# Rotary embedding at the eviction on VectorE, head norms with a scaled epsilon, and neighbourhood outputs folded out of PSUM

## The chip, the core and the metric

The kernel runs on one core of one Trainium2 chip. The time is the device time of one launch, in microseconds. Seven engines' records matter here: PE (TensorE matmul) and PEld (its weight loads), DVE (VectorE), ACT (ScalarE), POOL (GpSimd), SP (SyncE, which issues the DMAs), and the DMA queues themselves.

## What is computed

A trunk of two layers over 512 tokens (a grid of 8 rows by 64 columns) with 1024 channels in float32. Each layer adds three blocks to the residual stream, each behind an RMS norm: a mixer, a cross attention over 256 memory tokens, and a feed-forward block with a depthwise convolution. The change touches the mixer, which splits one input projection between eight heads of neighbourhood attention and grouped-query attention (eight query heads, two key heads, 64 channels each):

```python
proj = h @ w_in                                   # h = rms_norm(x)
na_q, na_k, na_v, g_q, g_k, g_v = split(proj)
na_out = neighbourhood_attention(na_q, na_k, na_v, rpb)
g_q = apply_axial_rope(rms_norm(g_q, q_norm), cos, sin)   # per head
g_k = apply_axial_rope(rms_norm(g_k, k_norm), cos, sin)
gqa_out = gqa_block_attention(g_q, g_k, g_v)
x = x + concatenate([na_out, gqa_out]) @ w_out

def rms_norm(x, g):
    return x * rsqrt(mean(x * x) + EPS) * g
def apply_axial_rope(x, cos, sin):                # halves x1, x2 of each axis
    return [x1 * cos - x2 * sin, x1 * sin + x2 * cos]
```

## The kernel before

Activations are held transposed: channels on the 128 partitions, the 512 tokens along the row. To keep float32 accuracy with TensorE's faster float32 replacement type, each operand is split in two parts, hi (a rounded copy, made on ACT) and lo (the rest, made on DVE or POOL), and a product is three matmuls: hi by hi, hi by lo, lo by hi. Every weight tile comes by DMA from SP's queue into a raw buffer, is cast to hi on ACT (line 265) and gets its lo on POOL or DVE (line 266), in two halves for most of the mixer's weights. There are four buffers of hi and lo, so a cast can wait for the matmuls that still read the weight four places before.

The RMS norm's factor of each token (`mix.rstd`, and `mix.rep`, the same spread over the partitions) is not put into the matmuls' operands; products are scaled by it as they leave PSUM.

*Order of the work.* PE, SP and a few other operations keep the order in which the program writes them. DVE, ACT and POOL are put in order by the tile scheduler, which has priorities and a simulated timeline; the order is fixed when the program is built, and each engine works through its own list in order. `behind(n)` shifts the priority of what it encloses.

*The mixer's loop.* Eight units of neighbourhood attention (four pairs of heads, two halves of the tokens each) are run by `weave`: in each round, transposes of the unit two rounds back, normalising of the one before, scores of the newest, and values of the unit two rounds back, with a piece of filler between. The filler is the rest of the input projection. For the grouped heads it is `gqa_project`, for k, q0, q1, v, q2, q3 in this order, each in two pieces of twelve matmuls; after that come the output projection and memory's keys and values. After the eight units, sixteen units of grouped attention follow in the same manner.

`Late` holds work to be done some pieces later: each piece is a tick, and `late(n, f)` runs f after n ticks.

*Values.* `na_values` multiplies with hi and lo of the probabilities side by side, and hi and lo of the values one below the other, so that a PSUM tile holds four parts to be added: two halves of the partitions, two along the row. Before, ACT copies the lower half (line 789), DVE adds it to the upper half for both parts (790), and a third addition in SBUF adds the two parts (791).

*Rotation.* `gqa_rope` takes the projected head pair out of PSUM (lines 840 to 842): ACT writes xs, the value by its gain, and its square, DVE writes cc, the value by gain and cosine. One piece later `swap` issues four DMAs that exchange the halves of xs into xr, sums the squares of each head by a matmul with `pairs`, and gets the variance on DVE (852, 855). Another piece later `rotate` has POOL take the power -1/2 (862), copy it into rows (863), multiply xr by the sine (864) and add cc (865). Two pieces later `norm` spreads the rows over the partitions by a matmul with the identity, and one piece later `split` multiplies xr by it (875) and makes the operands of the attention. The tables of cosine and sine are multiplied by `mix.rep` on POOL once in each layer (805), and the sums of squares by the square of `mix.rstd` (807).

Of the kernel before, what the change touches and what calls it, by code (L numbers as in the profile page):

```python
# [10 lines left out]
F32 = mybir.dt.float32  # L11
# [7 lines left out]
P = 128  # L19
# [154 lines left out]
def encoder_kernel(ctx: ExitStack, tc: tile.TileContext, t: dict, out: bass.AP):  # L174
# [203 lines left out]
    qkg = cpool.tile([P, DEPTH, 2], F32, name="qkg")  # L378
    gfin = cpool.tile([P, KC], F32, name="gfin")

    def load_parameters():
# [15 lines left out]
    def rsqrt(src, n, scale, factor=1.0):  # L397

        v = small(n)
        DVE.tensor_scalar(v, src, scale * factor, EPS * factor, op0=ALU.mult, op1=ALU.add)  # L400
        r = small(n)
        with behind(-40):
            POOL.tensor_tensor(r, v, mhalf[:, :n], op=ALU.pow)
        return r

# [10 lines left out]
    class Norm:  # L416
# [172 lines left out]
    for l in range(DEPTH):  # L589
# [185 lines left out]
        def na_values(u):  # L775
            p, bp = divmod(u, 2)
            pts = na.pop(u)
            if bp == 0:
                o32s[p] = tmp()
            th, tt = tmp((2, 2, P)), tmp((2, 2, P))  # L780
            for j in range(2):
                po = ps_mm().rearrange("p (i n q) -> p i n q", i=2, n=2)
                for i in range(2):
                    b = 2 * bp + i
                    for c in range(2):
                        PE.matmul(po[:, i], vblk[p // 2][WIN[b] + P * c][:, 2 * (p % 2) + j, :],
                                  pts[j][:, :, (2 * i + c) * P : (2 * i + c + 1) * P], start=c == 0, stop=c == 1)
                r = slice(64 * j, 64 * j + 64)
                ACT.copy(th[r], po[64:128])
                DVE.tensor_add(tt[r], po[0:64], th[r])  # L790
            DVE.tensor_add(o32s[p][:, 256 * bp : 256 * bp + 256].rearrange("p (i q) -> p i q", i=2), tt[:, :, 0], tt[:, :, 1])
            if bp == 1:
# [7 lines left out]

        gq, gk, gvt, gtab, r2 = [None] * 4, [], [], [], []

        def gqa_tables():
            for i in range(2):
                POOL.tensor_mul(gtab[0][:, i], gtab[0][:, i], mix.rep)
            r2.append(small(NB))
            POOL.tensor_mul(r2[0], mix.rstd, mix.rstd)

# [26 lines left out]
        def gqa_rope(g, pm):  # L835

            gain = qkg[:, l, 0:1] if g != "k" else qkg[:, l, 1:2]
            xs, sq, cc = tmp(), tmp(), tmp()
            with behind(-20):
                ACT.activation(xs, pm, AF.Copy, scale=gain)  # L840
                ACT.activation(sq, pm, AF.Square)
                DVE.scalar_tensor_tensor(cc, pm, gain, gtab[0][:, 0], op0=ALU.mult, op1=ALU.mult)  # L842

            def swap():
                xr = tmp()
                for i in range(4):
                    SP.dma_start(xr[32 * i : 32 * i + 32], xs[32 * (i ^ 1) : 32 * (i ^ 1) + 32])
                pv = ps_t()
                for b in range(NB):
                    PE.matmul(pv[:, 2 * b : 2 * b + 2], sq[:, b * P : (b + 1) * P], pairs, start=True, stop=True)  # L850
                v = small(2 * NB)
                DVE.tensor_tensor(v.rearrange("p (b j) -> p b j", j=2), pv[:, 0 : 2 * NB].rearrange("p (b j) -> p b j", j=2),
                                  r2[0].unsqueeze(2).to_broadcast([P, NB, 2]), op=ALU.mult)

                DVE.tensor_scalar(v, v, *((1.0 / HD, EPS) if g == "k" else (1.0, EPS * HD)), op0=ALU.mult, op1=ALU.add)
                late(1, lambda: rotate(xr, v))

            def rotate(xr, v):
                r = small(2 * NB)
                rows = tmp()  # L860
                with behind(-40):
                    POOL.tensor_tensor(r, v, mhalf[:, : 2 * NB], op=ALU.pow)
                    POOL.tensor_copy(rows.rearrange("p (b d) -> p b d", d=HD), r.unsqueeze(2).to_broadcast([P, 2 * NB, HD]))
                POOL.tensor_mul(xr, xr, gtab[0][:, 1])
                POOL.tensor_add(xr, cc, xr)
# [165 lines left out]
        def na_quanta(s):  # L1031
            if s == 3:
                gtab.append(rtile((2, S), F32))
                SP.dma_start(gtab[0], t["rope"])
                gqa_tables()
            return [NA_FILL] * 3
# [267 lines left out]
def _rope_tables():  # L1304

    tok = np.arange(S)
    col, row = tok // ROWS, tok % ROWS
# [69 lines left out]
```

## Time and profile before

| | |
|---|---|
| median of 3 runs | 1388.41 us (1386.73 to 1388.48) |
| the profiled execution | 1388.67 us |
| its span, first to last instruction | 1386.4 us |
| granted TensorE clock, mean | 0.992 of full speed |
| PE busy | 1355.3 us (98% of the span) |
| DVE, ACT, POOL busy | 838.3, 703.8, 719.7 us |

In the rows of the profile, `mm<-xg,hi` says which tiles an instruction writes and reads (mm, sc and tr are PSUM tiles; xg, r, t, s, hi, lo, raw are SBUF tiles), and L77 is a line of the kernel, which can be that of a helper. In a row of the timeline the first number is the start in us from the span's start, the second the duration; the bracket at its end is the idle time of the engine just before, and what ended it. In a row of groups the number behind x is how often it ran; then come the busy time in us, the mean of one in ns, and the idle time before them with what ended it. A float32 matmul with a plain float32 operand is recorded as two passes, so that four matmuls appear as eight. The clock (PEclk) is that granted to TensorE, as a share of full speed.

### The profile page before, as it was taken

Reading aid. Unit: us, or ns where it says so; the run is one execution under the profiler, and the core shown is the slowest. Engines: PE = TensorE matmul, PEld = TensorE weight load, DVE = VectorE, ACT = ScalarE, POOL = GpSimd, SP = SyncE. Lnnn points to the kernel's source line nnn. Section 1 sums busy time; section 2 is a strip of 40 time slices with the busy share of each in tenths; the row PEclk is TensorE's granted clock in tenths of the full one; section 3 lists DMA queues with packets and bytes.
Section 4 is the critical chain, followed back from the end, with each engine's and each line's share of the span. In section 5 each row is a group of like instructions: output and inputs, shape, how many; then the busy total and the mean of one; then the engine's idle time right before and its main releaser. Section 6 shows DMA issues by size and latency. Waiting matters only on the chain.

```text
span 1386.4 us, 19225 instructions
## 1 busy us (share of the span) xinstructions
PE 1355.3 (98%) x7072; PEld 1157.1 (83%) x7072; DVE 838.3 (60%) x1462; ACT 703.8 (51%) x1305; POOL 719.7 (52%) x537
## 2 busy tenths in 40 slices
PE   8999999999999999999999989999999999999997
PEld 7898789787888888888888978898788888888897
DVE  6666666363787187358446557754638833861874
ACT  6766577655443144234557657766654422432441
POOL 2458876635444444444645678756264444444441
PEclk9999999999999999999999999999999999999998
DMA  7753312322333333333356523223133333333331
GB/s 213 202 145 86 86 57 78 92 62 61 106 97 102 91 94 95 101 100 89 109 147 166 139 74 99 62 75 109 54 90 100 91 104 94 90 93 107 95 89 61
DMA packets 218205, 138.83 MB, mean 100 GB/s; under 512 B 6016, under 2 KB 211072, under 8 KB 218112
## 3 DMA queue, kind: packets, MB, share of 16 engines
q1 hardware_dynamic: 217968, 137.60, 34.9%
q8 instruction: 56, 0.92, 0.3%
q14 instruction: 37, 0.30, 0.1%
q10 hardware_dynamic: 144, 0.00, 0.0%
HBM read 125.00 MB, written 2.10 MB: 92 GB/s over the span
## 4 chain that ended last, share of the span: by engine, by line
PE 88%; ACT 4%; DVE 3%; POOL 2%; DMA 2%; issue 1%; SPq 0%; DVEq 0%; ACTq 0%; POOLq 0%
PE mm L77 79%; PE sc L77 5%; PE tr L64 3%; PE tr L77 1%; ACT hi L265 1%; DMA raw<-in_w_in 1%; POOL lo L266 1%; DMA raw<-in_w_down 1%; DVE s L900 1%; POOL r L266 0%; DMA xT<-in_xT 0%; ACT t L902 0%; DVE t L455 0%; DVE xg L473 0%; ACT t L745 0%
## 5 line engine op out<-in xcount | busy, mean ns | idle before, releaser
L266 POOL TENSOR_TENSOR lo<-raw,hi 128x1024 fp32r<-128x1024 f32 (+2 forms) x268 | 499.7, 1876 | 496.0 <-ACT hi L265 476.0
L77 PE MATMUL mm<-xg,hi 128*128 128x512 f32 x1920 | 595.5, 391 | 1.4 <-DVE t L842 1.4
L77 PEld LDWEIGHTS mm<-xg,hi 128*128 128x128 f32 x1920 | 357.4, 188 | 73.3 <-DVE t L842 1.6
L265 ACT CAST hi<-raw 128x512 fp32r<-128x512 f32 (+2 forms) x276 | 224.5, 837 | 349.0 <-PE mm L77 277.5
L77 PE MATMUL mm<-xg,lo 128*128 128x512 f32 x960 | 374.3, 390 | 0.0
L77 PE MATMUL mm<-r,hi 128*128 128x512 f32 (+1 forms) x1144 | 333.9, 376 | 4.4 <-ACT t L444 2.2
L77 PEld LDWEIGHTS mm<-r,hi 128*128 128x128 f32 x1144 | 209.2, 190 | 42.7 <-ACT t L444 3.1
L1202 DVE SCALAR_TENSOR_TENSOR t<-t,par,t 128x7 f32<-128x7 f32 (+1 forms) x352 | 201.9, 641 | 34.0 <-ACT t L1195 34.0
L77 PE MATMUL mm<-r,lo 128*128 128x512 f32 (+1 forms) x572 | 214.3, 375 | 0.0
L77 PEld LDWEIGHTS mm<-xg,lo 128*128 128x128 f32 x960 | 180.7, 188 | 38.1
L77 PEld LDWEIGHTS mm<-r,lo 128*128 128x128 f32 x572 | 108.5, 190 | 19.1
L1187 DVE TENSOR_TENSOR t<-mm,rep 128x512 f32<-128x512 f32 x88 | 60.1, 687 | 78.2 <-PE mm L77 62.3
L479 POOL TENSOR_SCALAR t<-t,s 128x512 f32<-128x512 f32 (+1 forms) x112 | 66.1, 607 | 75.1 <-DVE s L908 37.2
L1204 ACT ACTIVATE t<-t 128x512 f32<-128x512 f32 x44 | 27.9, 633 | 134.5 <-DVE t L1202 134.5
L1208 DVE TENSOR_TENSOR r<-t,r 128x512 fp32r<-128x512 f32 x44 | 90.5, 2056 | 7.3 <-ACT r L1207 4.1
L1231 DVE TENSOR_TENSOR xT<-xT,mm 128x512 f32<-128x512 f32 x32 | 21.9, 685 | 106.8 <-PE mm L77 106.8
L77 PE MATMUL sc<-r,r 128*128 128x256 f32 (+1 forms) x352 | 71.3, 334 | 0.4 <-ACT t L902 0.3
L64 PE MATMUL tr<-ident,t 128*128 128x128 f32 x456 | 63.3, 275 | 8.5 <-DVE r L473 2.8
L1195 ACT ACTIVATE t<-t,par 128x512 f32<-128x512 f32 x88 | 66.8, 806 | 3.2 <-DVE t L1187 3.2
L64 PEld LDWEIGHTS tr<-ident,t 128*128 128x128 f32 x456 | 52.0, 141 | 18.7 <-issue 6.9
L77 PE MATMUL mm<-r,r 128*128 128x256 f32 (+1 forms) x428 | 62.1, 297 | 0.1
L77 PEld LDWEIGHTS mm<-r,r 128*128 128x128 f32 x428 | 56.1, 191 | 2.7 <-POOL r L266 0.3
(155 smaller groups left out, 1598.8 us busy)
## 6 DMA issues: line engine op xcount, KB each, us to landing
raw<-in_w_up SPq DMA_DIRECT2D x88, 512.0 KB, 3.9
raw<-in_w_in SPq DMA_DIRECT2D x33, 512.0 KB, 4.5
raw<-in_w_down SPq DMA_DIRECT2D x32, 448.0 KB, 3.8
raw<-in_w_mem_kv SPq DMA_DIRECT2D x16, 512.0 KB, 3.9
raw<-in_w_down SPq DMA_DIRECT2D x16, 512.0 KB, 4.2
r<-in_bias SPq DMA_DIRECT2D x16, 384.0 KB, 6.2
r<-r SPq DMA_DIRECT2D x22, 256.0 KB, 5.3
raw<-in_w_out SPq DMA_DIRECT2D x8, 512.0 KB, 3.6
```

What stands on the lines that cost most here:

```text
L64: return lambda *a, **k: self.tc.keep_in_program_order(op(*a, **k))
L77: return self.tc.keep_in_program_order(self.engine.matmul(out, lhsT, rhs, **k))
L265: act.copy(hi[:, k], raw[:, k])
L266: (POOL if eng[0] == "P" else DVE).tensor_sub(lo[:, k], raw[:, k], f(hi)[:, k])
L479: eng.tensor_scalar(e, e, sums[:, col : col + 1], 1.0, op0=ALU.mult, op1=ALU.mult)
L900: DVE.tensor_reduce(nmx[:, c], sc[j], axis=AX.X, op=ALU.max, negate=True)
L1187: DVE.tensor_mul(u, us[side], ffn.rep)
L1195: ACT.activation(cc, u, AF.Identity, bias=par[:, l, CB + ch : CB + ch + 1], scale=w[1])
L1202: DVE.scalar_tensor_tensor(cc[:, dst], u[:, src], wi, cc[:, dst], op0=ALU.mult, op1=ALU.add)
L1204: ACT.activation(cs[0], cs[0], AF.Silu)
L1208: DVE.tensor_sub(acts[j][1], cs[0], f(acts[j][0]))
L1231: DVE.tensor_add(xT[m], xT[m], pm)
```

## The change

The signs of the sine table are exchanged between the halves, so that the sine is multiplied in before the halves change places. DVE now writes both xs (value by gain and sine) and cc from PSUM, and ACT only the square. `swap` issues the DMAs alone; the sums of the squares and the variance move into `rotate`, one piece later. The tables are no longer multiplied by the token's norm: since the head norm divides by the head's own size, the token's factor cancels but for the epsilon, which is multiplied by the token's variance instead (`geps`, made once in each layer by two operations on DVE). The variance then takes one operation on DVE instead of two. POOL keeps the power, the copy into rows and one addition for each group.

In `na_values` ACT copies only one of the two parts of the lower half, DVE adds the upper half's other part to it, and then the upper half's first part; both read PSUM, one after the other. As the diff has it, the copied part is the first of the lower half, the two parts of the upper half are added, and the lower half's second part, which multiplies lo by lo, is left out.

```diff
+    geps = cpool.tile([P, 2, NB], F32, name="geps")
...
         with behind(-40):
             POOL.tensor_tensor(r, v, mhalf[:, :n], op=ALU.pow)
-        return r
+        return r, v
...
-            self.rstd = rsqrt(pv[:, 0:nb], nb, 1.0 / D, factor)
+            self.rstd, self.var = rsqrt(pv[:, 0:nb], nb, 1.0 / D, factor)
...
-            th, tt = tmp((2, 2, P)), tmp((2, 2, P))
+            th = tmp((2, 2, P))
+            o32 = o32s[p][:, 256 * bp : 256 * bp + 256].rearrange("p (i q) -> p i q", i=2)
...
-                ACT.copy(th[r], po[64:128])
-                DVE.tensor_add(tt[r], po[0:64], th[r])
-            DVE.tensor_add(o32s[p][:, 256 * bp : 256 * bp + 256].rearrange("p (i q) -> p i q", i=2), tt[:, :, 0], tt[:, :, 1])
+                ACT.copy(th[r, :, 0], po[64:128, :, 0])
+                DVE.tensor_add(th[r, :, 1], po[0:64, :, 1], th[r, :, 0])
+                DVE.tensor_add(o32[r], po[0:64, :, 0], th[r, :, 1])
...
-        def gqa_tables():
-            for i in range(2):
-                POOL.tensor_mul(gtab[0][:, i], gtab[0][:, i], mix.rep)
-            r2.append(small(NB))
-            POOL.tensor_mul(r2[0], mix.rstd, mix.rstd)
+        def gqa_eps():
+            for i, e in enumerate((EPS, EPS * HD)):
+                DVE.tensor_scalar(geps[:, i], mix.var, e, None, op0=ALU.mult)
...
             with behind(-20):
-                ACT.activation(xs, pm, AF.Copy, scale=gain)
+                DVE.scalar_tensor_tensor(xs, pm, gain, gtab[0][:, 1], op0=ALU.mult, op1=ALU.mult)
+                DVE.scalar_tensor_tensor(cc, pm, gain, gtab[0][:, 0], op0=ALU.mult, op1=ALU.mult)
                 ACT.activation(sq, pm, AF.Square)
-                DVE.scalar_tensor_tensor(cc, pm, gain, gtab[0][:, 0], op0=ALU.mult, op1=ALU.mult)
             def swap():
                 xr = tmp()
                 for i in range(4):
                     SP.dma_start(xr[32 * i : 32 * i + 32], xs[32 * (i ^ 1) : 32 * (i ^ 1) + 32])
+                late(1, lambda: rotate(xr))
+
+            def rotate(xr):
                 pv = ps_t()
                 for b in range(NB):
                     PE.matmul(pv[:, 2 * b : 2 * b + 2], sq[:, b * P : (b + 1) * P], pairs, start=True, stop=True)
-                v = small(2 * NB)
-                DVE.tensor_tensor(v..., pv..., r2[0].unsqueeze(2).to_broadcast([P, NB, 2]), op=ALU.mult)
-                DVE.tensor_scalar(v, v, *((1.0 / HD, EPS) if g == "k" else (1.0, EPS * HD)), op0=ALU.mult, op1=ALU.add)
-                late(1, lambda: rotate(xr, v))
-
-            def rotate(xr, v):
-                r = small(2 * NB)
+                v, r = small(2 * NB), small(2 * NB)
+                DVE.scalar_tensor_tensor(v..., pv..., 1.0 / HD if g == "k" else 1.0,
+                    geps[:, int(g != "k")].unsqueeze(2).to_broadcast([P, NB, 2]), op0=ALU.mult, op1=ALU.add)
                 rows = tmp()
                 with behind(-40):
                     POOL.tensor_tensor(r, v, mhalf[:, : 2 * NB], op=ALU.pow)
                     POOL.tensor_copy(rows..., r.unsqueeze(2).to_broadcast([P, 2 * NB, HD]))
-                POOL.tensor_mul(xr, xr, gtab[0][:, 1])
                 POOL.tensor_add(xr, cc, xr)
                 late(2, lambda: norm(xr, rows))
...
-    tab = np.stack([np.concatenate([c, c, c, c]), np.concatenate([-s, s, -s, s])], axis=1)
+    tab = np.stack([np.concatenate([c, c, c, c]), np.concatenate([s, -s, s, -s])], axis=1)
```

More of the change, by code (lines that the diff above doesn't have):

```diff
@@ L797, in na_values @@
                     vblk[p // 2] = None
-        gq, gk, gvt, gtab, r2 = [None] * 4, [], [], [], []
-        def gqa_tables():
-            for i in range(2):
-                POOL.tensor_mul(gtab[0][:, i], gtab[0][:, i], mix.rep)
-            r2.append(small(NB))
-            POOL.tensor_mul(r2[0], mix.rstd, mix.rstd)
+        gq, gk, gvt, gtab = [None] * 4, [], [], []
+        def gqa_eps():
+            for i, e in enumerate((EPS, EPS * HD)):
+                DVE.tensor_scalar(geps[:, i], mix.var, e, None, op0=ALU.mult)
         def gqa_project(g):
@@ L850, in swap @@
                     PE.matmul(pv[:, 2 * b : 2 * b + 2], sq[:, b * P : (b + 1) * P], pairs, start=True, stop=True)
-                v = small(2 * NB)
-                DVE.tensor_tensor(v.rearrange("p (b j) -> p b j", j=2), pv[:, 0 : 2 * NB].rearrange("p (b j) -> p b j", j=2),
-                                  r2[0].unsqueeze(2).to_broadcast([P, NB, 2]), op=ALU.mult)
-                DVE.tensor_scalar(v, v, *((1.0 / HD, EPS) if g == "k" else (1.0, EPS * HD)), op0=ALU.mult, op1=ALU.add)
-                late(1, lambda: rotate(xr, v))
-            def rotate(xr, v):
-                r = small(2 * NB)
+                v, r = small(2 * NB), small(2 * NB)
+                DVE.scalar_tensor_tensor(
+                    v.rearrange("p (b j) -> p b j", j=2), pv[:, 0 : 2 * NB].rearrange("p (b j) -> p b j", j=2),
+                    1.0 / HD if g == "k" else 1.0, geps[:, int(g != "k")].unsqueeze(2).to_broadcast([P, NB, 2]),
+                    op0=ALU.mult, op1=ALU.add)
                 rows = tmp()
@@ L1034, in na_quanta @@
                 SP.dma_start(gtab[0], t["rope"])
-                gqa_tables()
+                gqa_eps()
             return [NA_FILL] * 3
```

## The prediction

> **What bounds the kernel now.** I read the page's busy shares and its chain first, then the chain in order of time, then windows of the two stretches where it leaves the matmuls, and there the timelines of PE and POOL.
>
> ```profile
> PE 1355.3 (98%) x7072; PEld 1157.1 (83%) x7072; DVE 838.3 (60%) x1462; ACT 703.8 (51%) x1305; POOL 719.7 (52%) x537
> PE 88%; ACT 4%; DVE 3%; POOL 2%; DMA 2%; issue 1%; SPq 0%; DVEq 0%; ACTq 0%; POOLq 0%
> 350.56 342.76 PE mm L77 x1512
> 835.30 0.92 PE sc L77 x4
> ```
>
> TensorE is the bound: a long stretch without a break does 1512 matmuls in 342.76 us, 0.227 us each, so a piece of twelve costs 2.72 us. The change adds and removes no matmul. It can only move time where PE waits, or where its clock is low after waiting. Those places are near the rotation:
>
> ```profile
> core 0: us, PE busy (x) PEld busy (x) DVE busy (x) ACT busy (x) POOL busy (x), PEclk, DMA share, GB/s
> 120.00:150.00 30.00, 26.64 (x149) 22.86 (x149) 18.88 (x34) 18.15 (x37) 23.59 (x22) 0.93 0.38 99
> 810.00:840.00 30.00, 26.76 (x145) 22.53 (x144) 17.90 (x31) 15.21 (x31) 23.13 (x22) 0.94 0.41 113
> ```
>
> POOL is busy 23 of 30 us there, and the clock falls to 0.93 and 0.94. PE's waits in layer 0 (times below 200) and layer 1, in brackets who ended them:
>
> ```profile
> 101.45 0.63 PE L64 MATMUL tr<-ident,t 128*128 128x128 f32 x4 [0.24 <-DVE s L852]
> 134.14 0.66 PE L64 MATMUL tr<-ident,t 128*128 128x128 f32 x4 [0.87 <-DVE r L473]
> 143.44 1.05 PE L77 MATMUL tr<-pairs,t 128*128 128x2 f32 x8 [1.26 <-ACT t L841]
> 146.75 2.08 PE L77 MATMUL mm<-ident,t 128*128 128x128 f32 x8 [1.24 <-POOL t L863]
> 148.48 1.20 PE L77 MATMUL mm<-r,hi 128*128 128x512 f32 x2
> 153.12 1.05 PE L77 MATMUL mm<-ident,t 128*128 128x128 f32 x8
> ...
> 801.46 0.73 PE L77 MATMUL mm<-xg,hi 128*128 128x512 f32 x2 [1.43 <-DVE t L842]
> 820.06 0.63 PE L64 MATMUL tr<-ident,t 128*128 128x128 f32 x4 [1.91 <-DVE r L473]
> 821.23 0.94 PE L77 MATMUL mm<-xg,hi 128*128 128x512 f32 x2
> 824.87 0.95 PE L77 MATMUL tr<-pairs,t 128*128 128x2 f32 x8
> 831.86 1.05 PE L77 MATMUL tr<-pairs,t 128*128 128x2 f32 x8 [1.33 <-ACT t L841]
> 838.78 1.15 PE L77 MATMUL mm<-ident,t 128*128 128x128 f32 x8
> ```
>
> The waits add up to 3.61 us and 4.67 us. From 821.23 to 824.87 the nine matmuls left of a piece take 3.64 us where 2.04 is usual: 1.6 us lost to a half-rate clock behind the 1.91 us wait. The spread in layer 0 costs 1.0 us (2.08 against 1.05) and more behind it.
>
> **The change, part by part.** The rows of the operations that it touches, and of their nearest kin:
>
> ```profile
> L842 DVE SCALAR_TENSOR_TENSOR t<-mm,qkg,r 128x512 f32<-128x512 f32 x10 | 7.5, 751 | 16.7 <-ACT t L841 14.6 <-POOL t L479 2.0
> L840 ACT ACTIVATE t<-mm,qkg 128x512 f32<-128x512 f32 x10 | 6.9, 695 | 0.1
> L841 ACT ACTIVATE t<-mm 128x512 f32<-128x512 f32 x10 | 6.0, 598 | 0.0
> L855 DVE TENSOR_SCALAR s<-s 128x8 f32<-128x8 f32 x10 | 4.6, 464 | 0.3
> L790 DVE TENSOR_TENSOR t<-mm,t 64x512 f32<-64x512 f32 x32 | 21.8, 683 | 10.7 <-ACT t L789 8.1 <-POOL t L479 1.5 <-POOL t L865 0.5
> L791 DVE TENSOR_TENSOR t<-t 128x256 f32<-128x256 f32 x16 | 9.7, 604 | 0.3
> L789 ACT COPY t<-mm 64x512 f32<-64x512 f32 x32 | 18.6, 583 | 6.1 <-PE mm L77 5.4
> L488 DVE TENSOR_TENSOR t<-mm,t 64x256 f32<-64x256 f32 x32 | 13.4, 418 | 11.2 <-ACT t L486 9.6 <-PE mm L77 0.7 <-PE tr L64 0.7
> L486 ACT COPY t<-mm 64x256 f32<-64x256 f32 x32 | 11.8, 369 | 4.3 <-PE mm L77 3.8
> L864 POOL TENSOR_TENSOR t<-t,r 128x512 f32<-128x512 f32 x10 | 12.9, 1295 | 3.4 <-DVE r L473 2.7 <-DMA t<-t 0.8
> L805 POOL TENSOR_TENSOR r<-r,rep 128x512 f32<-128x512 f32 x4 | 5.1, 1300 | 0.1
> ```
>
> *Engine totals.* POOL loses ten sine products (12.9 us), four table products (5.1) and two tiny squares. ACT loses ten evictions (6.9) and 32 x 0.21 us on smaller copies (583 against 369 ns for half the columns). DVE gains ten evictions of 0.75 us and four tiny products for the scaled epsilon, loses L855 (4.6), and per unit of neighbourhood values does 4 x 0.42 = 1.67 us where it did 2 x 0.68 + 0.60 = 1.97. None of these engines is the bound, so the totals are worth nothing by themselves. The epsilon products stand on DVE between the variance and the first scaling, which waits for the replicated norm anyway: nothing. If that cover were gone, two tiny operations a layer at L855's mean come to 4 x 0.46 = 1.9 us at most.
>
> *The values.* The chain that frees a product's PSUM tile was 0.58 + 0.68 = 1.27 us and is 0.37 + 2 x 0.42 = 1.20: nothing.
>
> *Eviction order.* The projection's PSUM tile is read by one engine after the other: before ACT, ACT, DVE (L842 waited 14.6 us for L841), now DVE, DVE, ACT. DVE no longer stands behind ACT, which begins with the weight cast at that moment. Three waits hang on that. 101.45: the sums' tile is read a piece later, and the transposes do not stand behind it: -0.24. 134.14 and 820.06: transposes wait for the split at L473, which stood behind L842 and so behind ACT's cast (1.14), 0.69 and 0.50. Now it stands behind two evictions, 1.5 us after the projection, and ACT's own half (cast, then a 0.6 us copy: 1.75). The split ends 2.4 us after the projection. In layer 0 PE gets there after some 2.8 us (turn, identity, values, four transposes): the 0.87 goes. In layer 1 there are no values between, PE gets there after 1.8: 0.7 of the 1.91 stays, -1.2, and with a wait no longer than layer 0's 0.87 I take the half rate behind it as gone: -1.6. Bounds of this pair: 0 to -3.5. 801.46: the tile is free after the square instead of after L842; ACT has the cast, a normalising copy of 0.4 and then the square, 2.8 us after the projection, where PE (two small groups and the values) is ready at 2.5: 0.3 stays, -1.1, bounds 0 and -1.4. The swap's four DMAs a group are issued in the same place of SP's queue, and what they read is ready earlier.
>
> *Sums a piece later.* The matmul over the squares, DVE's variance, POOL's power and the copy into rows now run two pieces ahead of the identity matmul that needs the rows, where there were three. For k and the first two q groups I find some 0.6 to 3 us to spare on POOL. The third q group is different: its sums come after the last projection piece, and on POOL, in the built program's order, its power now stands behind the pair of weight splits that this piece's end releases. Before, it had long run (first row below):
>
> ```profile
> 139.55 1.65 POOL L862 TENSOR_TENSOR s<-s,mhalf 128x8 f32<-128x8 f32 x1 [5.97 <-DVE s L855]
> 142.40 2.51 POOL L266 TENSOR_TENSOR lo<-raw,hi 128x512 fp32r<-128x512 f32 x2
> 150.76 1.36 POOL L479 TENSOR_SCALAR t<-t,s 128x512 f32<-128x512 f32 x2
> 829.65 1.29 POOL L500 TENSOR_TENSOR r<-t,r 128x512 fp32r<-128x512 f32 x1 [1.69 <-PE mm L77]
> 830.89 2.50 POOL L266 TENSOR_TENSOR lo<-raw,hi 128x512 fp32r<-128x512 f32 x2
> 833.33 0.62 POOL L863 COPY t<-s 128x512 f32<-128x512 f32 x1
> ...
> 141.05 1.14 ACT L265 CAST hi<-raw 128x512 fp32r<-128x512 f32 x2 [4.50 <-PE mm L77]
> 829.47 1.14 ACT L265 CAST hi<-raw 128x512 fp32r<-128x512 f32 x2
> ```
>
> The cast marks the end of the last piece, T: 141.05 and 829.47. Layer 0: half a cast 0.6, two splits 2.5, power 1.65, copy 0.62: rows at T + 5.4. PE has the sums, values and scores (0.8 + 0.9 + 0.92): it waits 2.7 us for the identity matmul. It waited 2.5 in two parts. The next identity matmul (fourth q group) hangs on POOL too: normalising 1.36, split 1.29, add 1.29, power, copy and some 0.4 of waiting for the normaliser's sums, at T + 12.0; or on PE at a low clock, T + 12.4. Before, it began at T + 12.07. One sum of 0.8 us has moved from before T to after it, so that compares with T + 12.87: -0.5, bounds -0.9 and +1. The low clock there I keep as it is.
>
> Layer 1: the split of the last neighbourhood output comes first, 1.25, then 2.5, 1.65, 0.62: rows at T + 6.0. PE has 0.8 + 0.92 + six matmuls 1.36 = 3.1: a new wait of 2.9 us in place of 1.33. The fourth group's rows follow after 1.38, 1.29, 1.65, 0.9 (two of memory's products now stand ahead) and 0.62: T + 11.85. Before, 838.78 - 829.47 = 9.31, and with the moved 0.8, 10.1: +1.75, bounds +0.5 and +2.5.
>
> *The clock behind that wait.* 1.91 us at 820.06 was followed by half rate at 1.6 us; 1.33 at 831.86 by none. 2.9 is nearer the first, but the second's surroundings (scores, output matmuls) are the ones that it has: 0 to 1.6, I take 0.8. [...]
>
> *Sum.* -0.24 - 0.87 - 0.5 - 1.1 - 1.2 - 1.6 + 1.75 + 0.8 = -3.0 us. The profiled execution took 1388.67 us (span 1386.4, 2.3 us around it), the median of the runs is 1388.41, 0.26 less. 1388.67 - 3.0 = 1385.7 against the profile, **1385.4** against the median.
>
> **Rivals.** *The clock holds behind the new waits.* Layer 1 loses no 0.8, and layer 0's half rate (2.08 for 1.05, then matmuls at 148.48 of 1.20 for 0.63, some 2.8 us in all) goes in part; for it speaks that 1.33 us cost no clock. POOL's chain to the fourth rows then is the bound, so only some of it counts: 1383 to 1384.6. [...]
>
> *Nothing changes.* The waits are only handed on: what is gained upstream is waited for at the third group's rows, since POOL's order there is fixed by the weight splits, or later, by the mixed stage of memory and grouped heads. For it: the sum is of eight terms of both signs. Against: the splits are released by PE and come earlier with it. 1388.4, within 1.5.
>
> *Slower: the rows come late for the second q group as well.* I have 0.6 us to spare there in both layers. If POOL is one split pair (2.5 us) behind, PE waits 1.9 us more in each, and with half rate behind them (1.6 each) that is +7.0: 1392.4. It decides against the change from some 1.5 us of lag in both layers. For it: POOL was at 23.6 of 30 us; against: 1.3 us a group leave that queue.
>
> **How the numbers follow.** 0.2% is 2.8 us, about what a measurement of this kernel can tell from none. The sum as taken 0.40: its own range is 1383.5 to 1387.5, a little over half beyond 0.2% (0.24) and the rest within (0.16). Clock holds 0.18, faster. Nothing changes 0.14. Slower 0.28, more than its margin says, because a tightened chain on a loaded in-order queue has more ways to be late than the one that I priced. Faster 0.42, same 0.30, slower 0.28. The range 1381.8 to 1392.0 reaches to the loss of both layers' low clock (-6.6) and most of the late second group.
>
> **What would show it.** PE's waits at L473, L842 and L841 of the list gone or under 0.8 us; the clock of layer 1's window at 818 to 825 full; a wait of 2.5 to 3 us at the identity matmul after the last projection in both layers, ended by POOL's copy; DVE's evictions ahead of ACT's square by 1.5 us. Wrong would be: identity waits also earlier, a clock under 0.9 in either window, or waits at the values.

## The result, and the profile after

The changed kernel took 1382.52 us (median of five runs, 1381.12 to 1384.26), the kernel before 1388.41 (1386.73 to 1388.80). By the medians that is 5.9 us less. The ratio, estimated from all the runs, is 0.9965, with a 95% interval of 0.9954 to 0.9976: 3.3 to 6.4 us faster. A second comparison, beside the experiments (e8 below), gave 0.9978, from 0.9967 to 0.9990. The forecast was 1385.4 us, faster, with a range of 1381.8 to 1392.0.

The profiled execution of the changed kernel took 1381.12 us, with a span of 1379.3. First its engine totals, from the page:

```profile
PE 1348.9 (98%) x7072; PEld 1153.1 (84%) x7072; DVE 836.7 (61%) x1482; ACT 691.4 (50%) x1295; POOL 701.4 (51%) x521
```

TensorE does the same 7072 matmuls in 1348.9 us where it took 1355.3. That is the first surprise of the page: its idle time (span less busy) has hardly moved, 1379.3 - 1348.9 = 30.4 us against 1386.4 - 1355.3 = 31.1. The matmuls themselves took 6.4 us less. Most of that is the clock: the profiled run has three stretches of 3.4 us at half clock fewer (the table below counts them), and at half clock such a stretch loses 1.7 us of matmul time, 5.1 us in all (worked out from one of before: from 251.33 to 254.74 us, 3.41 us, its granted clock was 0.50). The clock does not explain the other 1.3 us. The same two stretches as in the prediction, in the view of engine use by stretch (columns: stretch, length, busy time of each engine with its instructions, granted clock, DMA share, GB/s):

```profile
120.00:150.00 30.00, 25.77 (x157) 22.26 (x157) 18.61 (x35) 15.10 (x30) 22.95 (x22) 1.00 0.40 116
810.00:840.00 30.00, 25.11 (x139) 21.06 (x139) 19.24 (x34) 16.62 (x36) 22.35 (x27) 0.94 0.29 88
```

Layer 0's clock went from 0.93 to 1.00; layer 1's stayed at 0.94. Now PE's timeline, the rows of the rotation that begin with a wait (in brackets: idle time and who ended it):

```profile
143.01 1.16 PE L77 MATMUL mm<-ident,t 128*128 128x128 f32 x8 [2.59 <-POOL t L865]
149.44 1.16 PE L77 MATMUL mm<-ident,t 128*128 128x128 f32 x8 [1.64 <-POOL t L865]
...
813.23 0.66 PE L64 MATMUL tr<-ident,t 128*128 128x128 f32 x4 [0.57 <-DVE r L474]
826.24 1.16 PE L77 MATMUL mm<-ident,t 128*128 128x128 f32 x8 [2.66 <-POOL t L865]
```

Seven waits have become four: 8.28 us in the rotation of both layers before (3.61 + 4.67), 7.46 now (4.23 + 3.23). The waits for the projection's eviction and for ACT's square are gone. In their place PE waits for the third group's rows in both layers. POOL's timeline shows why, first layer 0, then layer 1:

```profile
138.14 2.54 POOL L266 TENSOR_TENSOR lo<-raw,hi 128x512 fp32r<-128x512 f32 x2 [2.92 <-ACT hi L265]
140.63 1.66 POOL L864 TENSOR_TENSOR s<-s,mhalf 128x8 f32<-128x8 f32 x1
142.35 0.61 POOL L865 COPY t<-s 128x512 f32<-128x512 f32 x1
...
820.13 1.28 POOL L501 TENSOR_TENSOR r<-t,r 128x512 fp32r<-128x512 f32 x1 [3.09 <-ACT r L500]
821.36 2.55 POOL L266 TENSOR_TENSOR lo<-raw,hi 128x512 fp32r<-128x512 f32 x2
823.87 1.65 POOL L864 TENSOR_TENSOR s<-s,mhalf 128x8 f32<-128x8 f32 x1
825.58 0.61 POOL L865 COPY t<-s 128x512 f32<-128x512 f32 x1
```

The power (L864) and the copy into rows (L865) stand behind the pair of weight splits (L266), after POOL had been idle for 2.92 us in layer 0 and 3.09 us in layer 1: the engine had time for them, but its inputs came too late.

### The profile page after: what moved, and what is told of

The parts are those of the page before. It is cut to its first block, busy times and chain, and to the rows that moved or that the text cites. A ratio compares the mean times of both kernels' runs of the same rounds, so it can differ in the third digit from the quotient of the medians.

```text
span 1379.3 us, 19221 instructions
## 1 busy us (share of the span) xinstructions
PE 1348.9 (98%) x7072; PEld 1153.1 (84%) x7072; DVE 836.7 (61%) x1482; ACT 691.4 (50%) x1295; POOL 701.4 (51%) x521
## 4 chain that ended last, share of the span: by engine, by line
PE 85%; DVE 2%; ACT 2%; POOL 1%; issue 0%; DVEq 0%; ACTq 0%; POOLq 0%
PE mm L77 77%; PE sc L77 4%; PE tr L64 3%; PE tr L77 1%; DVE xg L474 0%; DVE s L901 0%; ACT hi L265 0%; ACT xg L439 0%; DVE t L542 0%; POOL lo L266 0%; ACT t L903 0%; ACT t L1083 0%; ACT xg L473 0%; DVE r L1252 0%; POOL s L864 0%
## 5 line engine op out<-in xcount | busy, mean ns | idle before, releaser
L266 POOL TENSOR_TENSOR lo<-raw,hi 128x1024 fp32r<-128x1024 f32 (+2 forms) x268 | 498.9, 1874 | 513.3 <-ACT hi L265 507.5
```

The lines of the kernel that those rows point to most:

```text
L266: (POOL if eng[0] == "P" else DVE).tensor_sub(lo[:, k], raw[:, k], f(hi)[:, k])
```

## The experiments

The theory that the prediction left: the gain comes from the order of eviction (DVE first, no longer behind ACT's weight cast); the later sums lose some of it at the third group's rows; the fold and the epsilon are worth nothing. Rivals: the later sums carry the gain, or the fold does, or POOL's shorter work. Twelve runs were made, of ten new kernels, the changed kernel once more (e8) and e4 once more (e12), in groups of four (e1 to e4, e5 to e8, e9 to e12), each beside its own runs of the kernel before. That kernel took 1386.4 to 1387.0 us beside them, 1.4 to 2.0 us less than beside the changed kernel at first, so a forecast in us is better compared by its ratio to 1388.4. This is the key to all of them. "Waits" is the sum of PE's waits of 0.15 us and over in the profiled run, from the first group's sums to the fourth group's identity matmul, both layers together; "half rate" is the number of stretches of 3.4 us at half clock in it, ahead of the last 20 us.

| run | what it is | ratio to before (95%) | waits, us | half rate | profiled run, us |
|---|---|---|---|---|---|
| before | | 1 | 8.28 | 4 | 1388.67 |
| after | all parts | 0.9965 (0.9954 to 0.9976) | 7.46 | 1 | 1381.12 |
| e8 | all parts, again | 0.9978 (0.9967 to 0.9990) | 5.80 | 3 | 1382.21 |
| e1 | before + fold | 1.0017 (1.0008 to 1.0026) | 9.63 | 3 | 1387.62 |
| e2 | before + sine at eviction | 0.9962 (0.9949 to 0.9974) | 6.40 | 2 | 1382.07 |
| e3 | before + sums later | 1.0051 (1.0037 to 1.0064) | 10.44 | 4 | 1391.25 |
| e9 | before + fold + sine | 0.9968 (0.9955 to 0.9980) | 5.02 | 2 | 1380.39 |
| e10 | before + fold + sums later | 1.0078 (1.0066 to 1.0091) | 13.38 | 7 | 1397.84 |
| e5 | after without the fold | 1.0003 (0.9993 to 1.0013) | 8.75 | 6 | 1389.82 |
| e7 | after, ACT's square first | 1.0023 (1.0015 to 1.0032) | 11.19 | 2 | 1387.99 |
| e4 | after, all sums early | 0.9947 (0.9935 to 0.9960) | 4.34 | 1 | 1376.36 |
| e12 | e4 again | 0.9945 (0.9932 to 0.9957) | 6.01 | 1 | 1378.47 |
| e6 | after, third group's rows early | 0.9970 (0.9959 to 0.9981) | 6.45 | 4 | 1383.34 |
| e11 | after, only the fourth's sums late | 0.9972 (0.9962 to 0.9983) | 6.69 | 2 | 1384.38 |

Take the waits and 1.7 us a stretch off the profiled times, and 1370.1 to 1374.3 us are left in all fourteen, while the times themselves reach from 1376 to 1398. So these two columns carry most of what the kernels differ in. Part of what is left is the start: e4 and e11 have the same order of work on every engine for the first 140 us and reach the first identity matmul at 111.92 and 113.73 us.

### The order of eviction (e2, e7)

e2 gives the kernel before the sine's factor at the eviction and nothing else:

```
-                ACT.activation(xs, pm, AF.Copy, scale=gain)
-                ACT.activation(sq, pm, AF.Square)
-                DVE.scalar_tensor_tensor(cc, pm, gain, gtab[0][:, 0], ...)
+                DVE.scalar_tensor_tensor(xs, pm, gain, gtab[0][:, 1], ...)
+                DVE.scalar_tensor_tensor(cc, pm, gain, gtab[0][:, 0], ...)
+                ACT.activation(sq, pm, AF.Square)
...
-                POOL.tensor_mul(xr, xr, gtab[0][:, 1])
```

> The kernel before with the sine's factor at the eviction alone: both evictions on DVE ahead of ACT's square, no sine product on POOL; the sums stay a piece early, the epsilon and the tables' products as before. Theory: this part makes the gain upstream. PE's waits for the transposes' split (134.14: 0.87 us, 820.06: 1.91 us) shrink below 0.8 us, the half rate behind the second goes (1.6 us), the wait of 1.43 us at 801 goes; the third group's rows come before the splits as they did, so no wait of 2.6 us. 1388.4 - 4.8 = 1383.6 us, 1382 to 1385. Rival one (the sums a piece later make the gain): 1387.5 to 1389. Rival two (waits are only handed on to ACT's square, which now ends behind two DVE evictions): the waits for the square grow beyond 2 us in both layers, 1386 to 1389 us.

Measured: 1381.06 us against 1386.44 of before beside it, 5.4 us less. PE's timeline of e2 in layer 1, the places where before waited 1.43, 1.91 and 1.33 us:

```profile
797.11 0.73 PE L77 MATMUL mm<-xg,hi 128*128 128x512 f32 x2 [0.29 <-ACT t L842]
815.33 0.63 PE L64 MATMUL tr<-ident,t 128*128 128x128 f32 x4 [1.09 <-DVE r L473]
825.44 1.05 PE L77 MATMUL tr<-pairs,t 128*128 128x2 f32 x8 [1.23 <-ACT t L842]
```

The first two fell as forecast (the second to 1.09 us, not under 0.8), and the wait for ACT's square did not grow. Half rate did not follow the second any more, but it did follow the third (827.88 us). This one part alone gives as much as the whole change (0.9962 against 0.9965).

e7 takes the changed kernel and undoes the order alone; the sine stays at the eviction and off POOL:

```
+                ACT.activation(sq, pm, AF.Square)
                 DVE.scalar_tensor_tensor(xs, pm, gain, gtab[0][:, 1], ...)
                 DVE.scalar_tensor_tensor(cc, pm, gain, gtab[0][:, 0], ...)
-                ACT.activation(sq, pm, AF.Square)
```

> The changed kernel with one order undone: ACT's square of a projection is taken ahead of DVE's two evictions, so that these stand behind ACT's weight cast again; the sine's factor stays at the eviction. Theory: the order is what gains upstream, so waits like those of the kernel before come back: 0.9 us near 134, 1.4 us near 795, 1.9 us near 815 us, and the swap's DMAs come 1.5 us later. Against the changed kernel +3 to +6 us: 0.9985 to 1.001 of the kernel before. Rival (what gains is POOL without the sine product, not the order): 0.996 to 0.9975 of before, with those waits still under 0.8 us.

Measured: 1390.18 us against 1386.99, and 1383.65 for the changed kernel beside it (e8). Swapping two engines' turns at one PSUM tile costs 6.5 us. The groups of the changed kernel's evictions (busy time, mean ns, then the idle time ahead of them and what ended it), and DVE's first of e7:

```profile
L843 DVE SCALAR_TENSOR_TENSOR t<-mm,qkg,r 128x512 f32<-128x512 f32 x10 | 7.5, 751 | 11.8 <-PE mm L77 10.3 <-issue 1.4
L844 DVE SCALAR_TENSOR_TENSOR t<-mm,qkg,r 128x512 f32<-128x512 f32 x10 | 7.4, 740 | 0.0
L845 ACT ACTIVATE t<-mm 128x512 f32<-128x512 f32 x10 | 6.0, 600 | 2.9 <-DVE s L858 1.2 <-DVE t L844 0.8 <-issue 0.7
```

```profile
L844 DVE SCALAR_TENSOR_TENSOR t<-mm,qkg,r 128x512 f32<-128x512 f32 x10 | 7.5, 750 | 10.4 <-ACT t L843 10.4
```

PE's timeline of e7 in layer 1:

```profile
800.99 0.73 PE L77 MATMUL mm<-xg,hi 128*128 128x512 f32 x2 [1.28 <-DVE t L845]
820.22 0.63 PE L64 MATMUL tr<-ident,t 128*128 128x128 f32 x4 [2.55 <-DVE r L474]
```

In the changed kernel DVE's first eviction waits for PE, in e7 for ACT's square, and the waits of before are back in layer 1 (1.28 and 2.55 us for 1.43 and 1.91); in layer 0 0.53 us came back near 134 us where I had said 0.9. The rival that POOL's shorter work is what gains falls: e7 has that too.

### The sums a piece later (e3, e4, e12)

e3 moves only the sums, on the kernel before:

```
             def swap():
...
-                pv = ps_t()
-                (sums, variance)
-                late(1, lambda: rotate(xr, v))
+                late(1, lambda: rotate(xr))
+
+            def rotate(xr):
+                pv = ps_t()
+                (sums, variance)
```

> The kernel before with the sums, the variance and the power a piece later alone; evictions on ACT, ACT, DVE and the sine product on POOL as before. Theory: the transposes' waits of 0.87 and 1.91 us stay, the waits of 0.24 at 101 and of 1.26 and 1.33 us for the square go, and the third group's rows come behind the weight splits on POOL, with a wait of 2.5 to 3.5 us in both layers: 1388.4 - 0.2 + (0 to 3.3) = 1388 to 1391.5 us, 1390 the likeliest. Rival (the later sums carry the gain, because ACT's square is no longer waited for): 1383 to 1386 us.

Measured: 1392.84 us against 1386.44, 6.4 us more, and past the range that I gave, in us (1388 to 1391.5) and as a ratio (1.0051, where 1391.5 is 1.0022 of before). The mechanism was the one forecast, in layer 1 with 3.26 us at the third group's rows. What I had not seen is the first row, 1.96 us in layer 0:

```profile
125.79 0.66 PE L64 MATMUL tr<-ident,t 128*128 128x128 f32 x4 [1.96 <-DVE s L855]
...
833.95 1.59 PE L77 MATMUL mm<-ident,t 128*128 128x128 f32 x8 [3.26 <-POOL t L863]
```

The transposes and the sums take their PSUM tiles from the same two buffers. Once the sums come late, the second pair of transposes needs the buffer that DVE's variance has to read first, and that variance is behind other work in DVE's queue.

e4 is the changed kernel with all sums back in the swap's piece; the epsilon, the fold and the eviction stay:

```
             def swap():
...
-                late(1, lambda: rotate(xr))
+                v = sums()
+                late(1, lambda: rotate(xr, v))
```

> The changed kernel with the sums, the variance taken in the same piece as the swap's DMAs again, as before the change; all else as changed. Theory: the waits of 2.59 us and 2.66 us at the third group's rows shrink to about 1 us (the power stands ahead of the weight splits on POOL again, the copy into rows perhaps behind them), while waits of 0.5 to 1.3 us for ACT's square come back at the last group's sums: 1380 to 1382.5 us, 1381.5 the likeliest, against 1382.5 for the change. Rival (the later sums are what gains): 1384.5 to 1388 us.

e12 is the same kernel once more:

> The changed kernel with all sums early once more, beside the others of this call. Theory: 0.9935 to 0.996 of the kernel before again, and so 0.1 to 0.4% less than the changed kernel, whose two comparisons gave 0.9965 and 0.9978. Rival (the first comparison was lucky in its stretches of half rate): 0.9965 to 0.998.

Measured: 1379.05 against 1386.44, and again 1379.18 against 1387.04. Their intervals end at 0.9960 and 0.9957; those of the changed kernel begin at 0.9954 and 0.9967, so the first overlaps a little and the second does not. The later sums cost the change about 0.2 to 0.3%, some 3 us. PE's timeline of e4:

```profile
140.57 1.05 PE L77 MATMUL tr<-pairs,t 128*128 128x2 f32 x8 [1.18 <-ACT t L845]
148.48 1.16 PE L77 MATMUL mm<-ident,t 128*128 128x128 f32 x8 [0.55 <-POOL t L871]
...
811.45 0.63 PE L64 MATMUL tr<-ident,t 128*128 128x128 f32 x4 [1.04 <-DVE r L474]
821.60 1.05 PE L77 MATMUL tr<-pairs,t 128*128 128x2 f32 x8 [1.28 <-ACT t L845]
```

The third group's waits of 2.59 and 2.66 us are gone, those for ACT's square are back at 1.18 and 1.28. This is the fastest kernel of the study, and it is the one to keep.

### The fold (e1, e5, e10)

e1 gives the kernel before the fold alone:

```
-            th, tt = tmp((2, 2, P)), tmp((2, 2, P))
+            th = tmp((2, 2, P))
...
-                ACT.copy(th[r], po[64:128])
-                DVE.tensor_add(tt[r], po[0:64], th[r])
-            DVE.tensor_add(o32, tt[:, :, 0], tt[:, :, 1])
+                ACT.copy(th[r, :, 0], po[64:128, :, 0])
+                DVE.tensor_add(th[r, :, 1], po[0:64, :, 1], th[r, :, 0])
+                DVE.tensor_add(o32[r], po[0:64, :, 0], th[r, :, 1])
```

> The kernel before with one part of the change alone: the neighbourhood outputs folded out of PSUM by two additions that read PSUM, with the smaller copy on ACT. Theory (the gain comes from DVE no longer standing behind ACT at the projections' eviction): nothing, 1388.4 us within 0.8, the waits of PE at 134, 143, 147, 801, 820 and 832 us as before. Rival (the fold frees PSUM or DVE and carries the gain): 1383 to 1385 us.

Measured: 1389.26 us against 1386.44, a loss of 0.08 to 0.26%, where I had nothing. The profiled run shows 9.63 us of waits for 8.28, small ones for DVE's variance among them. The largest new one, 1.84 us at the fourth group's rows in layer 0, stands where before ran at half rate; nothing in the profile is large enough to name one cause. On the sine's kernel the fold makes no difference that the intervals tell (e9 below, 0.9968 against 0.9962).

e5 takes the fold out of the changed kernel (the same diff, backwards):

> The changed kernel with the neighbourhood values as they were before the change (a copy of both halves on ACT, one addition out of PSUM for each, one addition in SBUF); all else as changed. The fold alone cost 2.3 us on the kernel before. Theory: here too it gains nothing, so without it the time is that of the changed kernel or up to 2.3 us less: 0.9948 to 0.9967 of the kernel before, no new wait of PE. Rival (the change needs the fold: the larger copies delay ACT's square and with it the tile for the next projection): 0.998 to 1.000 of before, with waits for the square of over 1 us at 790 to 805 us.

Measured: 1387.59 against 1386.99. My theory fell: without the fold the changed kernel has no gain left. The rival was nearer, but its wait was 0.75 us at 803 us, not over 1 us, and the larger loss was elsewhere. DVE's timeline of e5 in layer 0:

```profile
122.90 1.38 DVE L791 TENSOR_TENSOR t<-mm,t 64x512 f32<-64x512 f32 x2 [2.14 <-PE mm L77]
125.65 0.16 DVE L857 SCALAR_TENSOR_TENSOR s<-tr,geps 128x8 f32<-128x8 f32 x1
```

PE's:

```profile
121.75 1.05 PE L77 MATMUL mm<-ident,t 128*128 128x128 f32 x8
...
125.86 0.65 PE L64 MATMUL tr<-ident,t 128*128 128x128 f32 x4 [1.78 <-DVE s L857]
```

and the changed kernel's DVE at the same work (the second of its four additions, and the variance):

```profile
118.61 0.42 DVE L792 TENSOR_TENSOR t<-mm,t 64x256 f32<-64x256 f32 x1
...
122.61 0.17 DVE L858 SCALAR_TENSOR_TENSOR s<-tr,geps 128x8 f32<-128x8 f32 x1
```

Without the fold the additions begin at 122.90 us, though ACT's copies had ended at 119.96; with it the second of them is at 118.61. They waited 2.14 us for PE and began as its identity matmul ended (121.75 + 1.05 = 122.80). That matmul reads the rows, a temporary from the same pool of twelve as the additions' second temporary (`tt`, which the fold removes); in the profile the additions' idle time was ended by PE here, and in the changed kernel by ACT alone. So the reading is that the later sums keep temporaries longer and the pool runs dry. DVE stands still, the variance behind it comes at 125.65, and PE's transposes wait 1.78 us. I did not change the pool's size by itself, so the wait is shown and the buffer behind it is inferred.

e10 has the edits of e1 and of e3 together on the kernel before:

> The kernel before with two other parts together: the fold and the sums a piece later; evictions on ACT, ACT, DVE and the sine product on POOL as before. The later sums alone gave 1.0051, with a wait of 1.96 us at 126 us for DVE's variance, which stood in DVE's queue behind the additions of the neighbourhood outputs. Theory: the fold's shorter copies bring those additions, and with them the variance, in time: that wait shrinks below 0.4 us, 1.002 to 1.004 of before. Rival (the fold only adds instructions to DVE, as alone, where it cost 0.17%): 1.0055 to 1.008, the wait still near 2 us.

Measured: 1397.05 against 1387.04, the rival's side and slower than all others. The wait that the fold was to remove stayed:

```profile
126.78 0.66 PE L64 MATMUL tr<-ident,t 128*128 128x128 f32 x4 [2.25 <-DVE s L856]
```

So the fold helps the late sums only where the other parts (DVE's eviction, the epsilon) are there too. In e10 DVE's additions stood still for 3.29 us ahead of this, and there for ACT's copies, which were behind ACT's weight cast.

### The epsilon (e9)

e9 has the edits of e1 and of e2 together on the kernel before, and so tells the epsilon's part when it is set against e4:

> The kernel before with two parts together: the fold of the neighbourhood outputs and the sine's factor at the eviction; sums early, the epsilon and the tables' products on POOL as before. It differs from the changed kernel with early sums (0.9947 of before) in the scaled epsilon alone. Theory (the scaled epsilon is worth nothing, the parts do not add because a wait taken away by one uncovers the next): 0.994 to 0.9962. Rival (the parts add, and the scaled epsilon is worth what is missing, 4.4 us): 0.9975 to 0.999.

Measured: 1382.50 against 1387.04, ratio 0.9968, between the two ranges. With the scaled epsilon and without the tables' products on POOL (e4, e12) it was 0.9947 and 0.9945. The intervals overlap at their ends, so it is likely but not certain that this part is worth some 3 us. Where they come from stays open: the two layers' waits are 5.02 us in e9, 4.34 and 6.01 in its partners, and e9 has one stretch of half rate more. Laid matmul by matmul beside e12's (the start of the same matmul in both), the profile of e9 loses 0.6 us ahead of 46 us, 0.7 in layer 0's mixer, nothing in layer 1's and 0.6 behind it, so no single wait that this part removes shows itself.

### The third and fourth groups' rows (e6, e11)

e6 moves the sums, the power and the copy of the third group alone a piece earlier, ahead of the weight splits on POOL:

```
+                rows = head_rows() if g == 2 else None
+                late(1, lambda: rotate(xr, rows))
```

> The changed kernel with the third query group's sums, variance, power and copy into rows a piece earlier, so that they stand ahead of the last projection's weight splits on POOL; the other groups as changed. Theory: the splits ahead of that power make the waits of 2.59 and 2.66 us. Both go; POOL's chain to the fourth group's rows gets 2.3 us shorter, so its wait of 1.64 us in layer 0 grows to 2 us at most and layer 1 gets one of 1 us at most. Against the changed kernel -3 to -5 us: 0.993 to 0.9945 of the kernel before. Rival (the wait is handed on to the fourth group's rows in full, POOL being the bound there): 0.996 to 0.997 of before, waits of 3 us and more at that group's identity matmul.

Measured: 1383.27 against 1386.99, the rival's number, with another place for the wait. Both third-group waits are gone, but POOL's program has a new order behind it, and the last neighbourhood output's split (L501) now comes behind the normaliser and the fourth group's power. POOL's row and PE's:

```profile
148.31 1.26 POOL L501 TENSOR_TENSOR r<-t,r 128x512 fp32r<-128x512 f32 x1
...
149.63 0.79 PE L77 MATMUL mm<-r,hi 128*128 128x512 f32 x1 [4.54 <-POOL r L501]
```

In the changed kernel that split began at 144.58 us. The 2.59 and 1.64 us of layer 0 were handed on as 4.54, and in layer 1 the fourth group's rows have a wait of 1.34 us that was not there.

e11 keeps the fourth group's sums late and has the others early (the condition in e4's edit is `g != 3`):

> The changed kernel with early sums for k and the first three query groups, and the sums of the fourth a piece later as changed. With all sums early PE waited 1.2 and 1.3 us for ACT's square at the fourth group's sums, and 0.55 us (layer 0) and nothing (layer 1) at its rows. Theory: the two waits for the square go, and the fourth group's rows come later by less than that in layer 1 and by 1 to 2 us in layer 0: 0.9935 to 0.996 of before, about as with all sums early. Rival (POOL's chain to the fourth group's rows takes all of it and more): 0.997 to 0.998, with a wait of 3 us or more there in both layers.

Measured: 1383.27 against 1387.04, the rival's ratio, though not by its wait of 3 us and more at the fourth group's rows: PE waits 0.87 and 0.85 us there. The waits for the square are gone, yet the third group's rows are late again, which I had not expected of a kernel that computes its power early:

```profile
143.88 1.16 PE L77 MATMUL mm<-ident,t 128*128 128x128 f32 x8 [1.75 <-POOL t L871]
829.38 1.16 PE L77 MATMUL mm<-ident,t 128*128 128x128 f32 x8 [1.89 <-POOL t L871]
```

The power ran ahead of the splits, but its copy into rows (L871) still stands behind them, and PE, which has neither the wait for the square nor the sums' 0.8 us ahead of it, is there earlier. What PE saves ahead of a POOL that sets the end it waits for there.

### The changed kernel once more (e8)

> The changed kernel itself once more, beside the others of this call. Its profiled execution had one stretch of half rate of 3.4 us (at 829 us, behind a wait of 2.66 us) and one at the end; the kernel before had stretches at 144, 250, 820 us and the end. Theory: a stretch comes or not with the same waits, so this execution has them in other places, or another number of them: one or two more or fewer. Rival (a stretch is tied to a wait's length): half rate again behind the 2.66 us wait and nowhere else but at the end. Time 0.9954 to 0.9976 of the kernel before.

Measured: 1383.65 us (twelve runs, 1380.21 to 1387.62) against 1386.99. At the third group's rows the waits are those of the first profile (2.58 and 2.65 us). The half rate is not: two stretches in layer 0 behind the 2.58 us wait, where the first profile had none behind 2.59, and again one in layer 1. So the theory's side, with two more. And the 1.64 us wait of layer 0 is gone: PE, at half rate, comes to the fourth group's matmul at 150.76 us, 1.5 us after POOL's copy ended. There a wait and a slow clock stand for each other. e4 and e12, one kernel, show the same: 0.55 us of waiting at that place behind a stretch of half rate, 2.22 without one.

## Why the prediction was right

The sign was right and the time within the range, 2.9 us above the median: 3.0 us less were forecast, 5.9 measured by the medians, 4.9 by the ratio. By its own steps:

- *Eviction order.* The mechanism is shown by e2 and e7. Counted from the start of each layer's mixer and without the sums that moved, the last projection piece ends 1.8 us earlier in layer 0 and 4.8 in layer 1 (forecast 1.1 and 3.9). 101.45 and 134.14 are gone as said. At 820.06 I kept 0.7 us, 0.57 was measured; at 801.46 I kept 0.3, nothing is left. The half rate that I took as gone behind 820.06 is gone.
- *Third group's rows.* T, the end of the last projection piece, is 137.45 and 820.17 us now. The rows came at T + 5.5 and T + 6.0 (forecast 5.4 and 6.0), PE's waits are 2.59 and 2.66 (2.7 and 2.9).
- *Fourth group.* Layer 0: T + 12.0, as said. Layer 1: POOL's copy ended at T + 11.7 (forecast 11.85), but PE at half rate came there at T + 13.2 (833.39 us). So the +1.75 and the +0.8 together were +3.1 against the 10.1 of before: the term of the clock was too small, because I took half of a stretch, and outside the last 20 us every stretch in the fourteen profiles is about 3.4 us long, or two together 6.8.
- *The low clock of layer 0 "I keep as it is".* In the profiled run it was gone, in e8's it was there. It is worth less than its length, because POOL's copy holds the place: the fourth group's matmul began at T + 12.0 with a full clock and a wait, and at T + 13.4 in e8 (150.76 - 137.33).
- *Where the sum ended.* It stopped at the fourth group's rows. Behind them, between 160 and 200 us, layer 0 gave 1.4 us of its gain back: PE waits 3.37 us there, ended by ACT and DVE, where it waited 1.96. e4 and e12, with early sums, do not have that.
- *What had no term.* Laid matmul by matmul beside each other, the two profiles differ by 7.1 us of span: 1.0 ahead of 46 us, 1.1 in layer 0's mixer (to 200 us), 1.6 at the stretch of half rate at 251 us, 2.4 in layer 1's mixer (to 870 us) and 1.1 behind it. So the two mixers gained 3.5 us where the sum had 3.0 (1.6 and 1.4), and in e8 2.2 (layer 1 2.4 again, layer 0 lost 0.2). The other half of the gain came from places where the forecast had nothing. At the start that is chance as far as the runs tell, since e4 and e11 differ there by as much as 1.8 us; at 251 us it is the clock, which fell well in the profiled run.
- *The rival with a clock that holds behind the new waits.* It held in layer 0 of the first profile, behind 2.59 us; the profiles of the changed kernel and of e8 otherwise go against it, with half rate behind 2.66 and 2.58 us.
- *"The values: nothing"* failed, though not on the kernel that it was costed for. I followed the PSUM tile and not the temporary that the fold gives back. On the kernel before the fold costs 0.17%; under the later sums and DVE's eviction it is worth 0.25 to 0.4%, which is the whole gain.
- *The epsilon: nothing, 1.9 us at most.* e9 against e4 and e12 puts it nearer 3 us of gain; the step looked at DVE's added operations and not at what leaving POOL's products out would bring. Not settled.
- *The slower rival*, late rows for the second group, did not come: PE had 0.7 us to spare there in both layers (0.6 forecast).

So the forecast was right for the reason it gave, the eviction's order, and near in size in the two mixers. Two things that it had at nothing weighed as much: the fold, without which the gain is gone (e5), and the clock, whose stretches come or not with the same waits. That the total lies as near as it does is in part luck.

## What to carry to other kernels

When two engines read one PSUM tile in turn, let the one go first that has nothing else due at that moment; here that order alone was worth what the whole change was. Delay an operation on an in-order queue only as far as the next big block that the same event releases, and count the buffers that live longer by it: parts of a change that are worth nothing alone can be what another part stands on. Compare PE's idle time and PE's busy time apart: if the same matmuls became cheaper, look at the clock first; that part of a gain varies from run to run (one to three stretches of half rate in the two profiles of the changed kernel).

## What the runs showed of the hardware

The half rate is the surprise. The kernel before and the changed kernel both wait at the same matmul in layer 0's later stage, for 1.95 and 1.94 us. First PE's row and the clock around it of before, then of after (columns as above, the clock stands ahead of the DMA share):

```profile
251.05 0.58 PE L77 MATMUL mm<-r,hi 128*128 128x512 f32 x1 [1.95 <-POOL r L492]
```

```profile
250.00:252.00 2.00, 0.95 (x3) 0.78 (x4) 0.00 (x0) 0.07 (x1) 2.00 (x3) 0.83 0.07 21
252.00:254.00 2.00, 2.00 (x7) 1.54 (x6) 1.33 (x3) 0.69 (x1) 1.47 (x2) 0.50 0.84 250
254.00:256.00 2.00, 2.00 (x9) 1.66 (x8) 0.72 (x2) 1.55 (x3) 0.42 (x1) 0.81 0.47 126
```

```profile
248.96 0.50 PE L77 MATMUL mm<-r,hi 128*128 128x512 f32 x1 [1.94 <-POOL r L493]
```

```profile
248.00:250.00 2.00, 1.04 (x5) 0.87 (x6) 0.27 (x1) 0.00 (x0) 2.00 (x3) 1.00 0.13 30
250.00:252.00 2.00, 2.00 (x10) 1.68 (x9) 1.87 (x3) 0.69 (x1) 1.40 (x2) 1.00 0.80 240
```

One is followed by half rate, the other by none. All fourteen profiles have this wait, at 1.94 or 1.95 us, and half rate followed in nine of them. A window of 2 us with h us of half rate has a mean clock of 1 - h/4, so the stretch of before is 4 x (0.17 + 0.50 + 0.19) = 3.44 us long and begins at 252 - 0.68 = 251.32. The other windows in which a stretch of before begins:

```profile
144.00:146.00 2.00, 1.52 (x9) 1.01 (x8) 1.94 (x5) 0.58 (x1) 2.00 (x2) 0.88 0.45 102
820.00:822.00 2.00, 1.94 (x10) 1.63 (x11) 1.17 (x2) 1.27 (x3) 0.00 (x0) 0.84 0.39 87
1376.00:1378.00 2.00, 0.83 (x6) 0.74 (x6) 0.71 (x3) 0.42 (x1) 0.13 (x1) 0.93 0.00 0
```

They give 145.52, 821.36 and 1377.72. In the 3.41 us ahead of a start, about as long as a stretch, PE was busy for 39% at 251.32, 44% at 821.36 and 63% at 145.52. That busy share does not tell either whether half rate follows, since a span of the same length at 45% (from 138.89 us of the changed kernel) and one at 52% (from 841.83 us of before) were followed by full clock. The span at 63% is half filled by the sums over `pairs`, matmuls whose result is two columns wide. The view by stretch of that span in the profile of before, first of all instructions, then of those with `pairs` (PE, PEld and DVE only):

```profile
142.11:145.52 3.41, 2.15 (x13) 1.57 (x12) 2.06 (x4) 2.42 (x5) 3.41 (x4) 1.00 0.21 48
142.11:145.52 3.41, 1.05 (x8) 0.97 (x8) 0.00 (x0) 1.00 0.21 48
```

The sums are 1.05 of its 2.15 us; whether they have a part in the half rate behind it was not tried. So with one and the same wait the half rate came in nine profiles and not in five, and neither the wait's length nor PE's busy share ahead of it tells which. What does was not shown.
